# Two RMS norms of a hybrid encoder block taken from turned squares instead of ones-matmuls, and the memory keys projected token by token

## The chip, the cores and the metric

The kernel runs on one core of a Trainium2 chip. The metric is the device time of one execution in microseconds (us), and the median of several executions is compared. The kernel before took 859.05 us (median of three, 858.74 to 859.78). Times with one decimal or two in the text are counted from the start of the profiled span.

## What is computed

One encoder block, on 512 tokens of width 1024, with a memory of 256 tokens that one of its three mixers attends to. All arrays are float32. Cut to what matters here:

```python
h = rms_norm(x, mix_norm_g)                    # x: 512 x 1024
ml_q, ml_k, ml_v, ml_o, gates, na_qkv, xa_q, merge = split(h @ w_in)
y_ml = mlstm_branch(...); y_na = neighbourhood_attention(...)
mem_k, mem_v = split(rms_norm(mem, mem_norm_g) @ w_mem_kv, 2)   # mem: 256 x 1024, each 256 x 512
y_xa = memory_cross_attention(xa_q, mem_k, mem_v)
x = x + (gated sum of the branches) @ w_out
a, u = split(rms_norm(x, ffn_norm_g) @ w_up, 2)                 # 2 x 2816 columns
x = x + (gelu(dwconv3(a, w_conv, b_conv)) * u) @ w_down
return rms_norm(x, final_norm_g)
```

`rms_norm(x, g)` is `x * rsqrt(mean(x*x, -1) + 1e-6) * g`. The factor `rsqrt(...)` is one number per token.

## The kernel before

**Three matmuls for one.** Every product with weights is done in three passes of a rounded format: each operand is a rounded part and a rest, and `mm3` (lines 334 to 337) issues high by high, high by rest and rest by high. A weight block arrives from memory (`emit_raw`, L214, the tiles `wr`, three buffers of 512 KB), is split by ScalarE (rounded part, L301) and VectorE (rest, L302) into tiles `w`, two halves for a block and four halves in all, and is then used by TensorE. `weights(key)` issues the load of the block three ahead and the split of the block one ahead. All loads go through the queue of SyncE (SP), which issues in program order and stands still at a load whose buffer isn't free.

**The order.** Blocks are worked off in the order of `block_list`: the mLSTM queries and keys, the token-major values, then `xaq` (four blocks), `o` (four), `memk` (four), `memv` (four), `naq`, `nak`, the gates and branches, `out` (eight), then `ua` and `uu` in turn (22 of each: the "up stage"), then the down projection. In between, generators with the mLSTM chunks, the memory attention and the neighbourhood attention are stepped on, so that small matmuls stand among the large ones. A scheduler then orders the instructions of each engine, so that an instruction can be moved ahead of others that were written before it.

**Norms.** The activations are channel-major (a channel per partition, a token per column), so the sum of squares of a token goes across partitions. ScalarE squares, the squares are added into an accumulator (`macc` of 128x256 for the memory on VectorE, `acc2` of 128x512 ahead of the up stage on GpSimd, L1267). `rstd_parts` (L421 to L424) folds the two halves of the partitions and splits the sum into two rounded parts; `rstd_cols` sums over the partitions by a matmul with ones (L431), takes the diagonal out by VectorE (L435) for a column per 128 tokens, raises it to the power -0.5 on GpSimd (L438), and builds a diagonal matrix of it (L447, L448); `rstd_row` multiplies ones by that matrix (L454) and so has the factors as a row on all partitions, which ScalarE copies out (L456). The tile with the row is `rb`.

**Memory keys.** `memk` is projected channel-major: for each of four blocks of 128 key channels, 24 matmuls with the weights as the stationary operand and 256 memory tokens as columns; VectorE multiplies by the row (`to_mk`, L1167). The memory's values are projected token-major: the memory tokens are stationary, 512 value channels are the columns, and ScalarE scales by the column on the way out (L1186).

**Up stage.** For each of 22 `f`, `pa` (from `ua`) is multiplied by `rb` into a padded tile (L520), a convolution of three taps follows (L522 to L524), then the gelu (L1293 to L1296), a second multiplication by the row on GpSimd (L1298), and the product with `pu` (L1304 or L1306). The accumulators `mm` have four buffers in PSUM, `at` four others. The first blocks `ua 0`, `uu 0`, `ua 1`, `uu 1` are multiplied before the row is there.

**Turning.** `turn_out` transposes a 128x512 tile on VectorE in squares of 32x32 (L169) and writes it to a scratch tensor in four DMAs (L172, `td`), whose rows complete the transposition; `turn_in` (L178, `U`) reads it back. The tag `nab` has two buffers; the turned mLSTM keys are read into it (`U`, one load per head, used by the copies L763 and L764), and later the biases of the neighbourhood attention.

Of the kernel before, what the change touches and what calls it, by code (L numbers as in the profile page):

```python
# [11 lines left out]
F32 = mybir.dt.float32  # L12
# [109 lines left out]
BCOLS = {n: (lambda k: P) for n in ("mlk", "o", "xaq", "memk", "naq", "nak", "g", "out", "ua", "uu")}  # L122
BCOLS.update({n: (lambda k: 512) for n in ("mlq", "memv")})
# [7 lines left out]
def hybrid_block(ctx, tc, xT, memT, wflat, vecs, gbias, nabias, out):  # L131
# [34 lines left out]
    def turn_out(src):  # L166

        t = scr()
        V.transpose(t.rearrange("p (j s a) -> p s j a", j=4, s=4), src.rearrange("p s (j b) -> p s j b", j=4))  # L169
        d = dp.tile([P, S], F32, name=nm("td"))  # L170
        for i in range(4):
            SY.dma_start(d[:, i * P:(i + 1) * P].rearrange("(j b) c -> b j c", j=4),  # L172
                         t[32 * i:32 * i + 32].rearrange("b (j c) -> b j c", j=4))
        return d

    def turn_in(d, tag, bufs, plain=False):
        u = tp.tile([P, S], F32, tag=tag, name=nm("U"), bufs=bufs)
        SY.dma_start(u, d)  # L178
        return u if plain else u.rearrange("p (i s a) -> p s i a", i=4, s=4)
# [861 lines left out]
    def xa_all(xq, mk, mv, yh, yl):  # L1041
# [3 lines left out]
        def prep(h):  # L1045
            q, k = (rt(), rt()), rt()
            split_act(q[0], q[1], xq[:, h * S:(h + 1) * S])
            k = (k[:, :M], k[:, M:])
            split_act(k[0], k[1], mk[:, h * M:(h + 1) * M])
            return q, k  # L1050
# [101 lines left out]
    for f in range(4):  # L1152
        if f == 2:
            mp = rstd_parts(macc, M)
        ps = proj(("o", f), NH, NL, at=mid({4: lambda: norm.append(rstd_cols(mp, M, "m"))} if f == 3 else {}))
        if f == 0:
            so.append(unit())
        g = so[0][:, f * S:(f + 1) * S]
        A.activation(g.rearrange("p (i s a) -> p s i a", i=4, s=4), ps.rearrange("p (s i a) -> p s i a", s=4, i=4),
                     AF.Tanh, scale=0.5)  # L1160
        V.tensor_scalar(g, g, 1.0, None, op0=ALU.add)
        step(RB / 2)
    mrc = norm[2][0]
    mkv = unit()
    mk, mv = mkv[:, 0:1024], mkv[:, 1024:2048]
    def to_mk(f, ps):
        V.tensor_tensor(mk[:, f * M:(f + 1) * M], ps[:, :M], norm[3], op=ALU.mult)  # L1167
# [8 lines left out]
    pss = [mmps() for _ in range(2)]  # L1176
    for i in range(4):
        ws = weights(("memv", i))
        for t in range(2):
            tsl = slice(t * P, (t + 1) * P)  # L1180
            for k in range(2):
                kk = 2 * i + k
                mm3(pss[t], MH[kk][:, tsl], ML[kk][:, tsl], ws[k][0], ws[k][1], kk == 0, kk == KT - 1)
        step(RM)
    for t in range(2):
        A.activation(mv[:, t * 512:(t + 1) * 512], pss[t], AF.Copy, scale=mrc[:, t:t + 1])  # L1186
# [87 lines left out]
    for f in range(FT):  # L1274
        if f == 0:
# [6 lines left out]
            p2 = rstd_parts(acc2, S)  # L1282
# [181 lines left out]
def _layout(inp):  # L1464
# [14 lines left out]
    for key, n in BLOCKS:  # L1479
# [16 lines left out]
        elif kind == "memk":  # L1496
            b = mkv[:, :, key[1] * P:(key[1] + 1) * P]
# [64 lines left out]
```

## Time and profile before

| what | value |
|---|---|
| median of three executions | 859.05 us |
| profiled execution | 858.86 us |
| its span (first to last instruction) | 857.1 us |
| TensorE busy, as the profile models it | 99% of the span |
| VectorE, ScalarE, GpSimd busy | 71%, 53%, 17% |
| memory stage (`memk` and `memv`) | 146.57 to 174.57 us |
| start of the up stage on TensorE | 496.30 us |
| last matmul | 849.66 us |

A row of the timeline gives start, duration, engine, line, operation, output and inputs, their shapes and the count; in brackets stands the idle time of the engine before it and what ended it. A matmul's shown duration includes its way through the pipeline, so what one matmul costs in a row of many is the distance from start to start.

### The profile page before, as it was taken

Reading aid. Unit: us, or ns where it says so; the run is one execution under the profiler, and the core shown is the slowest. Engines: PE = TensorE matmul, PEld = TensorE weight load, DVE = VectorE, ACT = ScalarE, POOL = GpSimd, SP = SyncE. Lnnn points to the kernel's source line nnn. Section 1 sums busy time; section 2 is a strip of 40 time slices with the busy share of each in tenths; the row PEclk is TensorE's granted clock in tenths of the full one; section 3 lists DMA queues with packets and bytes.
Section 4 is the critical chain, followed back from the end, with each engine's and each line's share of the span. In section 5 each row is a group of like instructions: output and inputs, shape, how many; then the busy total and the mean of one; then the engine's idle time right before and its main releaser. Section 6 shows DMA issues by size and latency. Waiting matters only on the chain.

```text
span 857.1 us, 12198 instructions
## 1 busy us (share of the span) xinstructions
PE 848.7 (99%) x4056; PEld 714.0 (83%) x4056; DVE 606.4 (71%) x1218; ACT 458.2 (53%) x965; POOL 148.3 (17%) x234
## 2 busy tenths in 40 slices
PE   9999999999999999999999999999999999999996
PEld 7898988988888888888888888888888888888885
DVE  6699677865458658997586557767766667756763
ACT  7465556775446648887644435444444444533442
POOL 2000200000102830454000212111111112110201
PEclk9999999999999999999999999999999999999999
DMA  8236734543335856888623432444433233844842
GB/s 273 83 114 208 240 138 146 196 149 110 124 109 173 230 142 199 227 235 238 206 89 109 147 111 96 150 148 147 148 99 99 98 98 112 255 111 138 242 101 99
DMA packets 74815, 131.55 MB, mean 153 GB/s; under 512 B 9976, under 2 KB 34936, under 8 KB 74752
## 3 DMA queue, kind: packets, MB, share of 16 engines
q1 hardware_dynamic: 64944, 120.25, 43.3%
q0 software_dynamic: 9664, 10.51, 6.4%
q8 instruction: 32, 0.52, 0.2%
q14 instruction: 31, 0.25, 0.1%
q10 hardware_dynamic: 144, 0.00, 0.0%
HBM read 116.03 MB, written 14.70 MB: 153 GB/s over the span
## 4 chain that ended last, share of the span: by engine, by line
PE 99%; DVE 0%; issue 0%; POOLq 0%; POOL 0%; ACT 0%
PE mm L336 28%; PE mm L335 28%; PE mm L337 28%; PE at L335 3%; PE at L336 3%; PE at L337 3%; PE at L983 1%; PE at L816 1%; PE at L818 1%; PE at L800 1%; PE at L950 0%; PE at L949 0%; PE at L760 0%; PE at L367 0%; POOLq L1557 0%
## 5 line engine op out<-in xcount | busy, mean ns | idle before, releaser
L335 PE MATMUL mm<-u,w 128*128 128x512 f32 (+1 forms) x912 | 353.7, 388 | 0.0
L336 PE MATMUL mm<-u,w 128*128 128x512 f32 (+1 forms) x912 | 352.2, 386 | 0.0
L337 PE MATMUL mm<-u,w 128*128 128x512 f32 (+1 forms) x912 | 352.1, 386 | 0.0
L301 ACT ACTIVATE w<-wr 128x512 fp32r<-128x512 f32 (+1 forms) x256 | 159.8, 627 | 132.8 <-PE mm L337 103.6
L302 DVE TENSOR_TENSOR w<-wr,w 128x512 fp32r<-128x512 f32 (+2 forms) x257 | 175.9, 688 | 70.1 <-ACT w L301 67.8
L337 PEld LDWEIGHTS mm<-u,w 128*128 128x128 f32 x912 | 171.4, 188 | 34.9 <-DVE w L302 0.4
L335 PEld LDWEIGHTS mm<-u,w 128*128 128x128 f32 x912 | 171.7, 188 | 33.7 <-ACT u L341 0.3
L336 PEld LDWEIGHTS mm<-u,w 128*128 128x128 f32 x912 | 171.5, 188 | 33.6 <-DVE u L342 0.5
L629 POOL DMA_DIRECT2D u<-nav_d x128 | 62.1, 494 | 102.3 <-PE at L983 53.5
L1298 POOL TENSOR_TENSOR s<-s,rb 128x512 f32<-128x512 f32 x21 | 35.8, 1702 | 180.2 <-DVE s L1296 172.5
L238 ACT ACTIVATE w<-u 128x512 fp32r<-128x512 f32 x49 | 30.8, 631 | 55.5 <-PE mm L337 42.3
L335 PE MATMUL mm<-w,u 128*128 128x512 f32 x148 | 57.8, 390 | 0.0
L336 PE MATMUL mm<-w,u 128*128 128x512 f32 x148 | 57.6, 389 | 0.0
L337 PE MATMUL mm<-w,u 128*128 128x512 f32 x148 | 57.6, 389 | 0.0
L238 DVE TENSOR_TENSOR w<-u,w 128x512 fp32r<-128x512 f32 x49 | 33.8, 690 | 31.4 <-ACT w L238 30.9
L337 PEld LDWEIGHTS mm<-w,u 128*128 128x128 f32 x148 | 27.8, 188 | 5.8
L335 PEld LDWEIGHTS mm<-w,u 128*128 128x128 f32 x148 | 27.8, 188 | 5.7
L336 PEld LDWEIGHTS mm<-w,u 128*128 128x128 f32 x148 | 27.8, 188 | 5.6
L341 ACT ACTIVATE u<-s 128x512 fp32r<-128x512 f32 x14 | 8.9, 632 | 36.1 <-DVE s L1306 36.1
L522 ACT ACTIVATE s<-pad,vec 128x512 f32<-128x512 f32 x30 | 24.4, 812 | 5.3 <-DVE pad L520 4.4
L238 POOL DMA_DIRECT2D u<-wflat x16 | 14.0, 900 | 67.4 <-DVE u L238 22.4
L523 DVE SCALAR_TENSOR_TENSOR s<-pad,vec,s 128x512 f32<-128x512 f32 x30 | 22.5, 749 | 4.0 <-ACT s L522 4.0
(297 smaller groups left out, 1134.2 us busy)
## 6 DMA issues: line engine op xcount, KB each, us to landing
wr<-wflat SPq DMA_DIRECT2D x124, 512.0 KB, 3.4
u<-wflat SPq DMA_DIRECT2D x48, 256.0 KB, 4.9
td<-s SPq DMA_DIRECT2D x160, 64.0 KB, 1.9
U<-td SPq DMA_DIRECT2D x40, 256.0 KB, 3.6
s<-xT SPq DMA_DIRECT2D x24, 256.0 KB, 3.9
nab<-nabias SPq DMA_DIRECT2D x16, 256.0 KB, 4.3
u<-nav_d POOLq DMA_DIRECT2D x128, 32.0 KB, 3.5
u<-wflat POOLq DMA_DIRECT2D x16, 256.0 KB, 6.3
```

Source lines behind the costliest of these rows:

```text
L238: chain[eng] = getattr({"V": V, "A": A, "G": G}[eng], what)(*a, **k).ins
L301: A.activation(h[:, u:v], src, AF.Copy)
L302: V.tensor_tensor(l[:, u:v], src, h[:, u:v].bitcast(F32), op=ALU.subtract)
L335: PE.matmul(ps, lh, rh, start=start, stop=False)
L336: PE.matmul(ps, lh, rl, start=False, stop=False)
L337: st["mm"] = PE.matmul(ps, ll, rh, start=False, stop=stop).ins
L341: A.activation(h, src, AF.Copy, scale=scale)
L522: A.activation(t1, pad[:, 0:512], AF.Identity, scale=vcol(w, i), bias=vcol(b, i))
L523: V.scalar_tensor_tensor(t1, pad[:, 1:513], vcol(w, n + i), t1, op0=ALU.mult, op1=ALU.add)
L629: G.dma_start(vw[r * 32:(r + 1) * 32, i * 256:(i + 1) * 256], nav_v[hf, r, CW[b]:CW[b] + 32, hp * 256:(hp + 1) * 256])
L800: PE.matmul(pv[:, i, 0:129], kt[:, d, i], va[:, i + d, h, 0:129], start=True, stop=True)
L1298: chain["G"] = G.tensor_tensor(c, c, rb2, op=ALU.mult).ins
```

## The change

`turn_out` and `turn_in` take tiles of any number of 128-token groups. Two new functions take the norm's factors from turned squares: `rstd_turned` reduces the turned accumulator over its columns on VectorE (one number per token and group), adds the epsilon and raises to -0.5 on GpSimd; `rstd_row_turned` writes these columns to a scratch tensor and reads it back on all partitions. The norm of the memory and the norm ahead of the up stage use them; the first norm of the kernel still goes through the ones-matmuls. The memory keys are projected like the values, scaled by the column, turned, and read back into `mkv`; the copies in `prep` of the memory attention pick a head's keys out of the turned layout. `pa1` and `pu1` of the up stage go into banks of `at`.

```diff
-BCOLS = {n: (lambda k: P) for n in ("mlk", "o", "xaq", "memk", "naq", "nak", "g", "out", "ua", "uu")}
-BCOLS.update({n: (lambda k: 512) for n in ("mlq", "memv")})
+BCOLS = {n: (lambda k: P) for n in ("mlk", "o", "xaq", "naq", "nak", "g", "out", "ua", "uu")}
+BCOLS.update({n: (lambda k: 512) for n in ("mlq", "memk", "memv")})
...
+    def rstd_turned(u, tag):
+
+        nt = u.shape[1]
+        v, col = tiny(nt), cp.tile([P, nt], F32, name=f"rc_{tag}")
+        V.tensor_reduce(v, u, axis=AX.XY, op=ALU.add)
+        V.tensor_scalar(v, v, 1.0 / D, EPS, op0=ALU.mult, op1=ALU.add)
+        G.tensor_tensor(col, v, nhalf[:, :nt], op=ALU.pow)
+        return col
+
+    def rstd_row_turned(col, tag):
+
+        d = dp.tile([S], F32, name=nm("rd"))
+        SY.dma_start(d.rearrange("(t p) -> p t", p=P), col)
+        rb = cp.tile([P, S], F32, name=f"rb_{tag}", tag=f"rb{S}", bufs=2)
+        SY.dma_start(rb, d.partition_broadcast(P))
+        return rb
...
-            split_act(k[0], k[1], mk[:, h * M:(h + 1) * M])
+            ms = mk.rearrange("p (t i s a) -> p s t i a", t=2, i=4, s=4)[:, h]
+            kh, kl = [x.rearrange("p (t i a) -> p t i a", t=2, i=4) for x in k]
+            A.activation(kh, ms, AF.Copy)
+            V.tensor_tensor(kl, ms, kh.bitcast(F32), op=ALU.subtract)
...
     for f in range(4):
-        if f == 2:
-            mp = rstd_parts(macc, M)
-        ps = proj(("o", f), NH, NL, at=mid({4: lambda: norm.append(rstd_cols(mp, M, "m"))} if f == 3 else {}))
+        if f == 0:
+            md = turn_out(macc.rearrange("p (s b) -> p s b", s=2))
+        elif f == 1:
+            mt = turn_in(md, "nab", 2)
+        elif f == 2:
+            mrc = rstd_turned(mt, "m")
+        ps = proj(("o", f), NH, NL, at=mid())
...
-    ps_m = [proj(("memk", 0), MH, ML, M)]
-    step(RM)
-    for f in range(1, 4):
-        ps_m.append(proj(("memk", f), MH, ML, M, at={4: lambda: norm.append(rstd_row(norm[2][1], M, "m"))} if f == 1 else {}))
-        for i in range(2 if f == 1 else 1):
-            to_mk(f - 1 + i if f == 1 else f, ps_m.pop(0))
-        step(RM)
...
+    kd2 = []
+    for name in ("memk", "memv"):
+        pss = [mmps() for _ in range(2)]
+        for i in range(4):
+            ws = weights((name, i))
+            for t in range(2):
+                tsl = slice(t * P, (t + 1) * P)
+                for k in range(2):
+                    kk = 2 * i + k
+                    mm3(pss[t], MH[kk][:, tsl], ML[kk][:, tsl], ws[k][0], ws[k][1], kk == 0, kk == KT - 1)
+            step(RM)
+            if name == "memv" and i == 2:
+                for t in range(2):
+                    SY.dma_start(mk[:, t * 512:(t + 1) * 512], kd2[t])
         for t in range(2):
+            if name == "memk":
+                m = scr()
+                A.activation(m, pss[t], AF.Copy, scale=mrc[:, t:t + 1])
+                kd2.append(turn_out(by4(m)))
+            else:
+                A.activation(mv[:, t * 512:(t + 1) * 512], pss[t], AF.Copy, scale=mrc[:, t:t + 1])
...
-            p2 = rstd_parts(acc2, S)
+            t2 = turn_in(turn_out(by4(acc2)), "nab", 2)
...
-            pa1 = proj(("ua", 1), HH, HL, at={2: lambda: norm.append(rstd_cols(p2, S, "2"))})
-            pu1 = proj(("uu", 1), HH, HL, at={3: lambda: norm.append(rstd_row(norm[4][1], S, "2"))})
-            rb2 = norm[5]
+            pa1 = proj(("ua", 1), HH, HL, bank=atps)
+            rb2 = rstd_row_turned(rstd_turned(t2, "2"), "2")
+            pu1 = proj(("uu", 1), HH, HL, bank=atps)
```

The scheduler makes the following of it. First the queue of SP at the start of the up stage, before. `s_5340` is the last tile of `x`; the tiles `wr` are the loads of `ua 2`, `uu 2`, `ua 3`, `uu 3` and `ua 4`.

```order
L1258 DMA s_5340<-xT 128x512
L214 DMA wr_5391<-wflat 128x1024
L214 DMA wr_5455<-wflat 128x1024
L214 DMA wr_5514<-wflat 128x1024
L214 DMA wr_5575<-wflat 128x1024
L214 DMA wr_5619<-wflat 128x1024
```

The same place in the change. `s_5393` holds the transposed squares, `U_5400` is the turned accumulator, `gf` are the gains of the last norm, `rd_5446` the scratch tensor of the factors and `rb_5448` the row.

```order
L1282 DMA s_5290<-xT 128x512
L232 DMA wr_5341<-wflat 128x1024
L173 DMA td_5395<-s_5393 32x4x128 x4
L179 DMA U_5400<-td_5395 128x512
L232 DMA wr_5408<-wflat 128x1024
L1349 DMA gf_7194<-gbias 128x512
L1349 DMA gf_7196<-gbias 128x512
L194 DMA rd_5446<-rc_5442 128x4x1
L232 DMA wr_5450<-wflat 128x1024
L196 DMA rb_5448<-rd_5446 128x512
L232 DMA wr_5507<-wflat 128x1024
L232 DMA wr_5551<-wflat 128x1024
```

Four writes and one read of the turning, and the write and the read of the row, now stand among the weights. The two loads of the gains, which before stand in the queue at the neighbourhood attention (issued at 421.0 and 421.5 us), have moved here, since they share the tag `nab` with the turned squares.

Second, VectorE at the point where the row is first used, before. `pad` are the products with the row for `f` 0 and 1; `w_5577` and `w_5580` are the halves of `uu 2`, `w_5621` is the first half of `ua 3`.

```order
L302 TENSOR_TENSOR w_5577<-wr_5455,w_5577 128x512
L520 TENSOR_TENSOR pad_148<-mm_5399,rb_5537 128x512
L520 TENSOR_TENSOR pad_151<-mm_5463,rb_5537 128x512
L523 SCALAR_TENSOR_TENSOR s_5552<-pad_148,vec,s_5552 128x512
L524 SCALAR_TENSOR_TENSOR s_5552<-pad_148,vec,s_5552 128x512
L302 TENSOR_TENSOR w_5580<-wr_5455,w_5580 128x512
L1294 SCALAR_TENSOR_TENSOR s_5556<-s_5556,s_5552 128x512
L523 SCALAR_TENSOR_TENSOR s_5564<-pad_151,vec,s_5564 128x512
L1296 SCALAR_TENSOR_TENSOR s_5552<-s_5556,s_5552 128x512
L524 SCALAR_TENSOR_TENSOR s_5564<-pad_151,vec,s_5564 128x512
L1304 SCALAR_TENSOR_TENSOR u_5381<-mm_5400,s_5552 128x512
L302 TENSOR_TENSOR w_5621<-wr_5514,w_5621 128x512
```

In the change the halves of `uu 2` are `w_5509` and `w_5512`, and the first half of `ua 3` is `w_5553`.

```order
L538 TENSOR_TENSOR pad_148<-mm_5349,rb_5448 128x512
L538 TENSOR_TENSOR pad_151<-at_5416,rb_5448 128x512
L541 SCALAR_TENSOR_TENSOR s_5484<-pad_148,vec,s_5484 128x512
L320 TENSOR_TENSOR w_5509<-wr_5408,w_5509 128x512
L542 SCALAR_TENSOR_TENSOR s_5484<-pad_148,vec,s_5484 128x512
L1318 SCALAR_TENSOR_TENSOR s_5488<-s_5488,s_5484 128x512
L541 SCALAR_TENSOR_TENSOR s_5496<-pad_151,vec,s_5496 128x512
L320 TENSOR_TENSOR w_5512<-wr_5408,w_5512 128x512
L1320 SCALAR_TENSOR_TENSOR s_5484<-s_5488,s_5484 128x512
L542 SCALAR_TENSOR_TENSOR s_5496<-pad_151,vec,s_5496 128x512
L1328 SCALAR_TENSOR_TENSOR u_5331<-mm_5350,s_5484 128x512
L320 TENSOR_TENSOR w_5553<-wr_5450,w_5553 128x512
```

The first half of `uu 2` stood ahead of the two products with the row and stands behind them now: one more split lies between the row and `ua 3`.

Third, the queue of SP ahead of the memory stage, before. `U` are the turned keys of the mLSTM heads 2 and 3 (head 1's stand five rows earlier), `R` rows for its scans, and the `wr` are `o 3` and `memk 0` to `memk 3`.

```order
L214 DMA wr_1366<-wflat 128x1024
L738 DMA R_1302<-rd 128x512
L178 DMA U_1798<-td_562 128x512
L214 DMA wr_1402<-wflat 128x1024
L738 DMA R_1499<-rd 128x512
L214 DMA wr_1464<-wflat 128x1024
L738 DMA R_1503<-rd 128x512
L178 DMA U_2065<-td_610 128x512
L738 DMA R_1790<-rd 128x512
L214 DMA wr_1552<-wflat 128x1024
L214 DMA wr_1642<-wflat 128x1024
```

In the change, with `td_1368` and `U_1409` the turned squares of the memory, `U_1515`, `U_1742` and `U_2015` the keys of heads 1 to 3, and `wr_1411` to `wr_1560` the blocks `memk 0` to `memk 2`:

```order
L756 DMA R_1302<-rd 128x512
L173 DMA td_1368<-s_1366 32x4x64 x4
L232 DMA wr_1411<-wflat 128x1024
L756 DMA R_1507<-rd 128x512
L179 DMA U_1409<-td_1368 128x256
L232 DMA wr_1472<-wflat 128x1024
L756 DMA R_1511<-rd 128x512
L179 DMA U_1515<-td_514 128x512
L179 DMA U_1742<-td_562 128x512
L232 DMA wr_1560<-wflat 128x1024
L179 DMA U_2015<-td_610 128x512
L756 DMA R_1734<-rd 128x512
```

The turned squares take one of the two `nab` buffers, and the keys of heads 1 and 2 are now read behind them; the key of head 2 takes the buffer that the squares leave.

More of the change, by code (lines that the diff above doesn't have):

```diff
@@ L166, in turn_out @@
     def turn_out(src):
-        t = scr()
-        V.transpose(t.rearrange("p (j s a) -> p s j a", j=4, s=4), src.rearrange("p s (j b) -> p s j b", j=4))
-        d = dp.tile([P, S], F32, name=nm("td"))
+        n = src.shape[1]
+        t = scr(n * P)
+        V.transpose(t.rearrange("p (j s a) -> p s j a", j=4, s=n), src.rearrange("p s (j b) -> p s j b", j=4))
+        d = dp.tile([P, n * P], F32, name=nm("td"))
         for i in range(4):
-            SY.dma_start(d[:, i * P:(i + 1) * P].rearrange("(j b) c -> b j c", j=4),
+            SY.dma_start(d[:, i * n * 32:(i + 1) * n * 32].rearrange("(j b) c -> b j c", j=4),
                          t[32 * i:32 * i + 32].rearrange("b (j c) -> b j c", j=4))
@@ L176, in turn_in @@
     def turn_in(d, tag, bufs, plain=False):
-        u = tp.tile([P, S], F32, tag=tag, name=nm("U"), bufs=bufs)
+        u = tp.tile([P, S], F32, tag=tag, name=nm("U"), bufs=bufs)[:, :d.shape[1]]
         SY.dma_start(u, d)
-        return u if plain else u.rearrange("p (i s a) -> p s i a", i=4, s=4)
+        return u if plain else u.rearrange("p (i s a) -> p s i a", i=4, a=32)
+    def rstd_turned(u, tag):
[11 more added lines that the diff above has]
+        return rb
     def by4(a):
@@ L1496, in _layout @@
         elif kind == "memk":
-            b = mkv[:, :, key[1] * P:(key[1] + 1) * P]
+            b = mkv[:, 2 * key[1]:2 * key[1] + 2, :512]
         elif kind == "memv":
```

13 lines of the change are left out of this document (removed).

## The prediction

> **What bounds the kernel now.** I read the page's busy times and its chain first, then what TensorE waited for, then TensorE's timeline from start to start.
>
> ```profile
> PE 848.7 (99%) x4056; PEld 714.0 (83%) x4056; DVE 606.4 (71%) x1218; ACT 458.2 (53%) x965; POOL 148.3 (17%) x234
> ...
> PEclk9999999999999999999999999999999999999999
> ...
> PE 99%; DVE 0%; issue 0%; POOLq 0%; POOL 0%; ACT 0%
> ```
>
> The chain that ended last is TensorE for 99% of the span, and the granted clock is full throughout. Busy time alone would not say that TensorE has no gaps, because the ends of matmuls are modelled. The waits do:
>
> ```profile
> PE at L367 <- DVE warm L363: 1.2, 1, 1.2
> ```
>
> That is the whole answer for TensorE: it waited 1.2 us, at its first instruction. So neither norm costs a stall today, and what the change can win is TensorE's own work. What it can lose is any new wait of TensorE.
>
> The price of a matmul is the distance from one start to the next.
>
> ```profile
> 157.09 0.28 PE L336 MATMUL mm<-u,w 128*128 128x256 f32 x1
> ...
> 159.72 0.28 PE L337 MATMUL mm<-u,w 128*128 128x256 f32 x1
> ```
>
> ```profile
> 518.51 0.39 PE L335 MATMUL mm<-u,w 128*128 128x512 f32 x1
> ...
> 529.39 0.39 PE L335 MATMUL mm<-u,w 128*128 128x512 f32 x1
> ...
> 534.83 0.39 PE L335 MATMUL mm<-u,w 128*128 128x512 f32 x1
> ...
> 535.28 0.39 PE L337 MATMUL mm<-u,w 128*128 128x512 f32 x1
> ```
>
> The first two rows are the second and the last of a `memk` block's 24 matmuls: 22 steps in 2.63 us, 0.1195 us each for 256 columns. The rows below them are the first matmuls of `ua 2`, `ua 3` and `uu 3`, the last two 24 steps apart: 5.44 us, 0.2267 us each for 512 columns; the row at 535.28 is the third matmul of `uu 3`. Twice 0.1195 is 0.239, so a wide matmul saves 0.0123 us against two narrow ones.
>
> **The change part by part.** *Memory keys.* 4 x 24 = 96 matmuls of 256 columns become 4 x 12 = 48 of 512: 96 x 0.1195 = 11.47 us against 48 x 0.2267 = 10.88 us, **-0.59 us**. The small matmuls between the blocks stay where they were.
>
> The Trainium skill (TensorE: Matmul & The Clock Gate, "Back-to-back issue gap") gives an isolated gap of N/2.4 + 2.5 ns, so that halving the count would save only 48 x 2.5 = 0.12 us. By it, the keys would give -0.12 in place of -0.59; the two distances above leave some 13 ns per matmul here, not 2.5, and I take the trace.
>
> *Ones-matmuls.* Four go, two of 256 and two of 512 columns.
>
> ```profile
> 508.54 0.39 PE L431 MATMUL at<-s,onesr 128*128 128x512 f32 x1
> 508.76 0.39 PE L335 MATMUL mm<-u,w 128*128 128x512 f32 x1
> ```
>
> ```profile
> 152.22 0.28 PE L454 MATMUL at<-s,onesr 128*128 128x256 f32 x1
> 152.34 0.28 PE L335 MATMUL mm<-u,w 128*128 128x256 f32 x1
> ```
>
> Each takes its place in the row of matmuls and no more: 0.22 and 0.12. Together 2 x 0.227 + 2 x 0.12 = **-0.69 us**. The sum is -1.28 us.
>
> *What VectorE, ScalarE and GpSimd lose and gain* (folds, diagonals, `to_mk` out; transposes, two reductions, two key copies on ScalarE in) is worth nothing by itself: TensorE waited for none of them. It matters only where a weight half is split too late, which I follow at the two places where a new wait stands.
>
> *Up stage: when is the row there?* The last addition of squares, then the pieces of the turning as they are elsewhere in this trace:
>
> ```profile
> 498.09 1.29 POOL L1267 TENSOR_TENSOR acc<-acc,s 128x512 f32<-128x512 f32 x1 [4.07 <-ACT s L1266]
> ```
>
> ```profile
> L169 DVE STREAM_TRANSPOSE s<-s 128x512 f32<-128x512 f32 x24 | 16.9, 707 | 2.9 <-ACT s L962 2.2
> ...
> L1066 DVE TENSOR_REDUCE y<-at 128x2 f32<-128x512 f32 x8 | 5.5, 686 | 0.0
> ...
> L956 DVE TENSOR_SCALAR y<-y 128x2 f32<-128x2 f32 x16 | 2.6, 164 | 0.2
> ```
>
> ```profile
> 171.87 1.77 SPq L172 DMA_DIRECT2D td<-s  x4
> 173.73 0.38 SPq L214 DMA_DIRECT2D wr<-wflat  x1
> 175.25 0.34 SPq L178 DMA_DIRECT2D U<-td  x1
> ```
>
> ```profile
> 506.68 1.43 DVE L302 TENSOR_TENSOR w<-wr,w 128x512 fp32r<-128x512 f32 x2 [1.97 <-ACT w L301]
> ```
>
> ```profile
> 510.35 1.04 POOL L438 TENSOR_TENSOR rc<-y,nhalf 128x4 f32<-128x4 f32 x1 [10.97 <-DVE y L435]
> ```
>
> ```profile
> td<-s SPq DMA_DIRECT2D x160, 64.0 KB, 1.9
> U<-td SPq DMA_DIRECT2D x40, 256.0 KB, 3.6
> ...
> R<-rd SPq DMA_DIRECT2D x8, 256.0 KB, 3.8
> ...
> vec<-vecs SPq DMA_DIRECT2D x1, 86.0 KB, 6.2
> ...
> vec<-vecs ACTq DMA_DIRECT2D x1, 4.0 KB, 3.2
> ```
>
> The sum is complete at 498.09 + 1.29 = 499.4. The transpose ends at 500.2, the four writes and their landing take 175.25 - 171.87 = 3.4 (503.6), the read 3.6 (507.2). In the new order of VectorE the reduction stands between the two halves of `uu 1`, which are split at 506.68 and behind; so it runs at 507.4 and ends at 508.1, the second half is done at 508.8, the small addition at 509.0, the power at 510.1. Then the factors are written, in time X, and read back as a row; that is the kind of read `R` is (a row of 512 onto all partitions), 3.8 us. The row is used from 510.1 + X + 3.8 + 0.1 = 514.0 + X.
>
> X has no row of its own: 128 partitions with four single numbers each, written to places apart. Its bounds from the rows are 1.9 (`td`, 128 runs of 512 bytes) and four times that, 7.6, if each of the 512 numbers costs what a run of `td` costs. The nearest row by size and shape of run is the 4 KB transfer of 32 bytes per partition, 3.2 us; I take **X = 3.2**, the row at 517.2.
>
> The Trainium skill (DMA: Bandwidth & Descriptors, "Rules for kernel authors") says that a last dimension with strides becomes one descriptor per element and should be rearranged. That speaks against this write: 512 descriptors for 2 KB. No run so far shows such a transfer.
>
> *Until when may the row come?* Before:
>
> ```profile
> 516.41 1.28 DVE L520 TENSOR_TENSOR pad<-mm,rb 128x512 f32<-128x512 f32 x2
> ```
>
> ```profile
> 513.70 0.68 DVE L302 TENSOR_TENSOR w<-wr,w 128x512 fp32r<-128x512 f32 x1
> ```
>
> ```profile
> 530.97 0.68 DVE L302 TENSOR_TENSOR w<-wr,w 128x512 fp32r<-128x512 f32 x1
> ```
>
> The second row is the end of `ua 2`'s split. The row of factors is used first at 516.41, and behind it VectorE works without a long pause until the halves of `ua 3` and `uu 3` are split. The tightest is the first half of `uu 3`, done at 530.97 + 0.68 = 531.65 and wanted by its third matmul at 535.28: 3.6 us to spare. In the change that matmul comes 0.45 earlier (two ones-matmuls of this stage gone; what is gone earlier moves both alike), and one more split, 0.68, stands behind the row. So the row may be later than 516.41 by 3.6 - 0.45 - 0.68 = 2.5 us, that is at **518.9**, before TensorE waits. At 517.2 there are 1.7 us to spare: cost nothing. The accumulators don't decide: with `pa1` and `pu1` in `at`, `ua 2` and `uu 2` have their own banks, where before `ua 2` at 518.5 needed the bank that L520 frees at 517.1.
>
> SP stands still while it waits for X. Behind it is the load of `uu 3`, whose buffer isn't free before the split of `ua 2` (513.70 + 0.68 before), and whose use is 20 us off. It hides.
>
> *Memory stage.* The keys of head 2 now wait for the buffer of the turned squares, and on VectorE and ScalarE their copies stand ahead of the split of `memk 0`.
>
> ```profile
> 125.24 0.42 DVE L558 TENSOR_TENSOR acc_m<-acc_m,s 128x256 f32<-128x256 f32 x1
> ```
>
> ```profile
> 122.00:134.00 12.00, 12.00 (x61) 10.17 (x60) 10.05 (x26) 9.93 (x28) 0.00 (x0) 1.00 0.48 174
> ```
>
> ```profile
> 141.17 0.68 DVE L302 TENSOR_TENSOR w<-wr,w 128x512 fp32r<-128x512 f32 x1
> ```
>
> ```profile
> 146.57 0.36 PE L335 MATMUL mm<-u,w 128*128 128x256 f32 x1
> ```
>
> The sum is complete at 125.7. The window's columns are its length and then the busy time of TensorE, of its weight loads, of VectorE, ScalarE and GpSimd: VectorE is 10.05 of 12 us busy there, so I give the transpose until 127.5; writes 3.4, read 3.6, reduction 0.4: 135. The keys are read by 138.6 and copied by 139.5, when the split of `memk 0` began at 141.17 before anyway. It is wanted at 146.4, so some 5 us cover the new wait. The two folds, the diagonals and ScalarE's three small copies no longer stand ahead of `memk 1`. The keys' way back (two key copies, turning, read) ends some 10 us behind the last `memk`, at about 170, while the memory attention starts after `nak`. Cost nothing.
>
> **The sum.** 858.86 of the profiled execution, whose span is 857.1, less 1.28 is 857.6. The median of before is 0.19 above that execution, which would give 857.8. I predict 857.6.
>
> **Rivals.** *The row is late (slower).* Above X = 4.9 TensorE waits by the excess, at `uu 3`; at X = 6.2, which is what the slowest load on this queue took, the wait eats the 1.3 us; at X = 7.6 the row comes at 521.6, TensorE waits 2.7 and the time is 857.6 + 2.7 = 860.3. Against it speaks that 2 KB are moved; for it, that 512 separate numbers are written to memory, which nothing in this kernel did. Beyond X = 8 the kernel is slower by over 0.2%. Should each number cost three times as much as a run of `td`, X is 22.8, the row at 536.8, the wait 17.9 and the time 875.5.
>
> The Trainium skill (VectorE: DVE Perf Modes, "The three transpose paths") warns that a plain copy that transposes by strides is 19 times slower than the transposing path. By that figure on `td`'s 1.9 us X would be 36 us, an estimate, and the time near 889; no row here bears it out.
>
> *The memory's turning is late.* The two rows below are the least, the median and the longest landing of all writes of `td` and of all reads `U`.
>
> ```profile
> DMA to landing us min/median/max: 1.6/1.9/4.6
> ```
>
> ```profile
> DMA to landing us min/median/max: 2.6/3.6/5.5
> ```
>
> If one write of `td`, the read and the keys' read take their longest, the keys come 2.7 + 1.9 + 1.9 = 6.5 us later, at 145.1; their copies take 0.9 and the split 0.7, so the half is there at 146.7 where it is wanted at about 146.4. TensorE waits 0.3 to 0.4 us for `memk 0`: 858.0.
>
> *The matmuls don't get cheaper.* If the wide matmuls with the memory tokens as stationary operand were no better than two narrow ones, only the ones-matmuls would go: 858.2. The `memv` blocks already run this way at the distance of 0.2267, which speaks against it.
>
> **How the numbers follow.** Forecast without a new wait: 0.68, of which 0.18 lies beyond -0.2% (1.7 us; -1.28 is near that bound, and 0.2% is about what a measurement of this kernel tells from no change). Late row with X up to 7.6: 0.10, within 0.2%. Late row beyond that, up to three times a run and more: 0.14, slower. Memory's turning late: 0.06; matmuls no cheaper: 0.02; both within 0.2%. Faster 0.18, same 0.50 + 0.10 + 0.06 + 0.02 = 0.68, slower 0.14. The range goes from 1 us below the forecast (the spread of the three runs before) to the late row at X = 7.6: 856.6 to 860.3. It leaves out the case of 0.14.
>
> **What would show it.** In the profile of the changed kernel TensorE's answer on waits should still hold one entry; 48 matmuls of 512 columns should stand in `memk` at 0.2267 apart; each of the two ones-matmul lines should occur once; the write of the factors should land in about 3.2 us, and the products with the row start at about 517 less the 1 us gained earlier. A TensorE wait on VectorE's split at `uu 2` to `ua 4` would show the late row; one at the first `memk` block the late keys.

## The result and the profile after

The changed kernel takes 866.11 us (median of four, 865.47 to 867.87) beside 859.41 for the kernel before on the same chips: the ratio is 1.0081, with a 95% interval of 1.0069 to 1.0093. It is slower by 6.7 us. 857.6 was predicted, 856.6 to 860.3. The profiled execution took 867.87, its span is 866.1.

I read the same views in the same order. The chain that ended last of the changed kernel:

```profile
PE 94%; DMA 2%; issue 1%; DVE 1%; POOL 0%; ACT 0%; POOLq 0%; SPq 0%
```

TensorE is no longer the whole chain: 2% of it is transfers, in a kernel whose chain had none. Then what TensorE waited for (total, times, longest):

```profile
PE mm L353 <- ACT w L319: 5.5, 1, 5.5
PE at L385 <- DVE warm L381: 1.2, 1, 1.2
PE mm L355 <- DVE w L320: 0.9, 2, 0.5
```

The wait at the start is the old one. New is one wait of 5.5 us on ScalarE's half of a weight split, with two small ones on VectorE's half behind it. The next fences follow the first backwards: TensorE's timeline, ScalarE's, VectorE's and the queue of SP.

```profile
523.24 0.39 PE L355 MATMUL mm<-u,w 128*128 128x512 f32 x1
529.08 0.79 PE L353 MATMUL mm<-u,w 128*128 128x512 f32 x1 [5.45 <-ACT w L319]
529.67 0.63 PE L354 MATMUL mm<-u,w 128*128 128x512 f32 x1
530.10 0.65 PE L355 MATMUL mm<-u,w 128*128 128x512 f32 x1
```

```profile
527.69 0.81 ACT L540 ACTIVATE s<-pad,vec 128x512 f32<-128x512 f32 x1 [14.28 <-DVE pad L538]
528.41 0.61 ACT L319 ACTIVATE w<-wr 128x512 fp32r<-128x512 f32 x1
```

```profile
526.91 0.69 DVE L538 TENSOR_TENSOR pad<-mm,rb 128x512 f32<-128x512 f32 x1 [12.77 <-DMA rb<-rd]
```

```profile
510.44 0.38 SPq L194 DMA_DIRECT2D rd<-rc  x1
510.87 0.50 SPq L232 DMA_DIRECT2D wr<-wflat  x1
521.90 0.33 SPq L196 DMA_DIRECT2D rb<-rd  x1
```

The block `uu 2` starts 5.6 us after `ua 2` ends (523.24 + 0.23). Its weights are split at 528.41, because on ScalarE that split stands behind the convolution of `f` = 0 (L540), which waits for the product with the row (L538), which waits for the row until 526.9. And the row is late because its write is issued at 510.44 and the read only at 521.90. The landing times (last number, us from issue):

```profile
rb<-rd SPq DMA_DIRECT2D x1, 256.0 KB, 5.0
...
rd<-rc SPq DMA_DIRECT2D x1, 2.0 KB, 11.4
```

The 2 KB take 11.4 us to land. The weight load issued behind them at 510.87, that of `ua 3`, is slow too; it landed at 523.6, some 5 us before `ua 3` would have been due without the stall:

```profile
DMA to landing us min/median/max: 12.8/12.8/12.8
```

There is a second cost behind the wait. In these windows the column after the busy times is the granted clock:

```profile
523.00:529.00 6.00, 0.63 (x3) 0.19 (x1) 1.75 (x3) 1.31 (x2) 0.00 (x0) 0.97 0.47 133
529.00:532.00 3.00, 2.92 (x7) 2.16 (x8) 2.25 (x4) 1.38 (x4) 0.00 (x0) 0.50 0.01 3
532.00:536.00 4.00, 4.00 (x19) 3.31 (x18) 2.80 (x6) 2.18 (x4) 1.74 (x1) 1.00 0.39 120
```

For 3 us behind the stall the clock is at half: 7 matmuls where 13 fit at 0.2267. Those steps of 0.43 take 1.5 us more than steps of 0.2267. The Trainium skill (TensorE: Matmul & The Clock Gate, "What's actually happening") says that the clock falls to half after an idle window of some 3.4 us and comes back after a busy one of that length. This trace agrees, with 5.45 us idle and 3 us at 0.50; two runs below differ, where waits of 3.3 us (`write_act`) and 2.9 us (`pe_warm`) were enough.

Matched matmul by matmul with the kernel before, TensorE is 0.19 us late when `ua 2` begins and 9.0 us late at the last matmul. 8.8 us arise in the up stage: 5.6 at `uu 2`, 1.5 by the clock, and 1.5 at the third matmuls of `ua 3` and `uu 3` with the step behind each; some 0.2 are spread over slightly longer steps. That the 0.19 are not -1.28 comes mostly from this execution's first weights, on which TensorE goes in steps of 0.43 until 9.8 us (+1.36). In the profiled executions of the kernels below, whose first stage is the same, it lies between 0.1 us early and 1.4 late at that point: this part varies from one execution to the next.

### The profile page after: what moved, and what is told of

Same layout as the page of the kernel before. It is cut to its first block, busy times and chain, and to the rows that moved or that the text cites. A ratio compares the mean times of both kernels' runs of the same rounds, so it can differ in the third digit from the quotient of the medians.

```text
span 866.1 us, 12075 instructions
## 1 busy us (share of the span) xinstructions
PE 851.1 (98%) x4004; PEld 712.6 (82%) x4004; DVE 601.5 (69%) x1192; ACT 455.1 (53%) x955; POOL 149.0 (17%) x234
## 4 chain that ended last, share of the span: by engine, by line
PE 94%; DMA 2%; issue 1%; DVE 1%; POOL 0%; ACT 0%; POOLq 0%; SPq 0%
PE mm L355 27%; PE mm L353 27%; PE mm L354 27%; PE at L353 3%; PE at L354 3%; PE at L355 3%; DMA rd<-rc 1%; PE at L1001 1%; PE at L834 1%; PE at L836 1%; PE at L818 1%; DMA wr<-wflat 1%; PE at L967 0%; PE at L968 0%; PE at L778 0%
## 5 line engine op out<-in xcount | busy, mean ns | idle before, releaser
L353 PE MATMUL mm<-u,w 128*128 128x512 f32 x864 | 339.6, 393 | 5.7 <-ACT w L319 5.5
L355 PE MATMUL mm<-u,w 128*128 128x512 f32 x864 | 338.1, 391 | 0.9 <-DVE w L320 0.9
L354 PE MATMUL mm<-u,w 128*128 128x512 f32 x864 | 337.9, 391 | 0.0
L353 PEld LDWEIGHTS mm<-u,w 128*128 128x128 f32 x864 | 163.2, 189 | 39.0 <-ACT w L319 5.9
L355 PEld LDWEIGHTS mm<-u,w 128*128 128x128 f32 x864 | 162.8, 188 | 36.5 <-DVE w L320 2.4
L354 PEld LDWEIGHTS mm<-u,w 128*128 128x128 f32 x864 | 163.2, 189 | 33.4 <-DVE u L360 0.5
L353 PE MATMUL mm<-w,u 128*128 128x512 f32 x164 | 64.3, 392 | 0.0
L355 PE MATMUL mm<-w,u 128*128 128x512 f32 x164 | 63.8, 389 | 0.0
L354 PE MATMUL mm<-w,u 128*128 128x512 f32 x164 | 63.8, 389 | 0.0
L540 ACT ACTIVATE s<-pad,vec 128x512 f32<-128x512 f32 x30 | 24.3, 812 | 24.1 <-DVE pad L538 22.9
L355 PEld LDWEIGHTS mm<-w,u 128*128 128x128 f32 x164 | 30.8, 188 | 6.5
L354 PEld LDWEIGHTS mm<-w,u 128*128 128x128 f32 x164 | 30.8, 188 | 6.3
L353 PEld LDWEIGHTS mm<-w,u 128*128 128x128 f32 x164 | 30.8, 188 | 6.1
L538 DVE TENSOR_TENSOR pad<-mm,rb 128x512 f32<-128x512 f32 x21 | 14.5, 692 | 16.6 <-DMA rb<-rd 12.8
```

Of the source, the lines that this page charges most:

```text
L353: PE.matmul(ps, lh, rh, start=start, stop=False)
L354: PE.matmul(ps, lh, rl, start=False, stop=False)
L355: st["mm"] = PE.matmul(ps, ll, rh, start=False, stop=stop).ins
L538: V.tensor_tensor(pad[:, 1:513], ps, rbt, op=ALU.mult)
L540: A.activation(t1, pad[:, 0:512], AF.Identity, scale=vcol(w, i), bias=vcol(b, i))
```

## Experiments

All times are medians where no other number of executions is given. `mem_only`, `row16`, `write_act` and `pe_warm` ran beside the kernel before at 859.09; `runs128`, `write_twice`, `defer` and `defer_act` beside 858.96.

**The memory's part alone** (`mem_only`). The up stage has its old norm again:

```diff
-            t2 = turn_in(turn_out(by4(acc2)), "nab", 2)
+            p2 = rstd_parts(acc2, S)
...
-            pa1 = proj(("ua", 1), HH, HL, bank=atps)
-            rb2 = rstd_row_turned(rstd_turned(t2, "2"), "2")
-            pu1 = proj(("uu", 1), HH, HL, bank=atps)
+            pa1 = proj(("ua", 1), HH, HL, at={2: lambda: norm.append(rstd_cols(p2, S, "2"))})
+            pu1 = proj(("uu", 1), HH, HL, at={3: lambda: norm.append(rstd_row(norm[2][1], S, "2"))})
+            rb2 = norm[3]
```

> The memory's turned norm and the token-by-token keys stay, the up stage has its old norm with folds and ones-matmuls. Theory (the whole loss is the up stage's row of factors, which comes 9 us later than I took): nothing is left of the loss; TensorE has its wait at the start and no other, and the memory stage gains 0.59 by 48 wide matmuls and 0.24 by two ones-matmuls of 256 columns, so 0.8 us less than the kernel before, some 858.6 beside 859.4. Rival (the memory's part costs as well): TensorE waits in the memory stage, and the time is above 860.

Measured: 858.52, ratio 0.9993 (0.9985 to 1.0002). No wait in the memory stage; one of 0.5 us on the first weights, at 9 us. So the whole loss belongs to the up stage, and the memory's part is free of waits, as theory had it. The time by itself can't tell 0.8 us from nothing; the gain is read from rows. From the first small matmul ahead of the keys to the first of the values, in the kernel before and in the changed one:

```profile
144.43 0.38 PE L816 MATMUL at<-u,E 128*128 128x129 f32 x2
...
161.33 0.48 PE L335 MATMUL mm<-w,u 128*128 128x512 f32 x1
```

```profile
145.59 0.38 PE L834 MATMUL at<-u,E 128*128 128x129 f32 x2
...
161.82 0.48 PE L353 MATMUL mm<-w,u 128*128 128x512 f32 x1
```

16.90 against 16.23 us: 0.67 less, for the keys and one of the two ones-matmuls (0.71 predicted).

**The same 2 KB in longer runs** (`row16`). Each partition gets four neighbouring tokens, so that the factors lie in memory as 128 runs of 16 bytes:

```diff
-            t2 = turn_in(turn_out(by4(acc2)), "nab", 2)
+            t2 = turn_in(turn_out(acc2.rearrange("p (b s) -> p s b", s=4)), "nab", 2)
...
-        SY.dma_start(d.rearrange("(t p) -> p t", p=P), col)
+        SY.dma_start(d.rearrange("(p t) -> p t", p=P), col)
```

> As the changed kernel, but the up stage's squares are turned so that each partition holds the sums of four neighbouring tokens; the factors are then written as 128 runs of 16 bytes in place of 512 single numbers, the same 2 KB. Theory (the write is paid by the piece; 512 pieces took 11.4 us to land): 128 pieces land in 3 to 4 us, the row is used at about 518.5 where it was 526.9, no wait of TensorE is left, the weight load behind the write lands in under 6 us where it took 12.8, and the time is 858.1, 1.3 below the kernel before. Rival (the write is slow for its place in the queue, between loads): it still takes 8 us or more, and the time is above 862.

Measured: 857.99, ratio 0.9989 (0.9980 to 0.9998), 1.1 us less than the kernel before. Its waits, its two transfers and its first product with the row:

```profile
PE at L385 <- DVE warm L381: 1.2, 1, 1.2
```

```profile
rb<-rd SPq DMA_DIRECT2D x1, 256.0 KB, 4.4
...
rd<-rc SPq DMA_DIRECT2D x1, 2.0 KB, 2.7
```

```profile
516.97 0.69 DVE L538 TENSOR_TENSOR pad<-mm,rb 128x512 f32<-128x512 f32 x1 [4.12 <-DMA rb<-rd]
```

Two access patterns are all that differs, the orders of VectorE and ScalarE are the same, and TensorE has only its wait at the start. The shape of the write made the whole loss. That it is the number of pieces, as this expectation said, did not hold; the probes below show it.

**The write on another queue** (`write_act`). The write is issued by ScalarE:

```diff
-        SY.dma_start(d.rearrange("(t p) -> p t", p=P), col)
+        nc.scalar.dma_start(d.rearrange("(t p) -> p t", p=P), col)
```

> As the changed kernel, but the write of the 512 factors is issued on ScalarE's queue and not on SP's, so that no load stands before or behind it in its own queue. Theory (pieces): it still lands after about 11 us, the row is used at 526 to 527 and the time stays at 865 to 866; only the weight load that stood behind the write on SP's queue may land earlier. Rival (shared queue): the write lands in 2 to 4 us, and the time falls to about 858.

Measured: 865.16, ratio 1.0066 (1.0052 to 1.0079). The write, a window in which it is under way (last columns: clock, busy share of the DMA engines, GB/s), and the wait at `uu 2`:

```profile
rd<-rc ACTq DMA_DIRECT2D x1, 2.0 KB, 10.5
```

```profile
514.00:521.00 7.00, 7.00 (x32) 5.79 (x32) 0.02 (x1) 0.00 (x0) 0.00 (x0) 1.00 0.00 0
```

```profile
PE mm L353 <- ACT w L319: 3.3, 1, 3.3
```

Shared queue, the rival, is out. The window says more: while the write was outstanding, the DMA engines are recorded at a share of 0.00. They were not busy working off pieces then. They had done so before: from 510 to 514 us the record has 528 packets on this queue, and from 514 until the landing at 520.8 it has no packet of any queue.

```profile
q10 hardware_dynamic: 528, 0.00, 7.4%
```

So the 10.5 us lie for the most part between the last packet and the signal of the landing. The row came 2.2 us earlier than in the changed kernel (524.70), and TensorE's wait is 2.2 us shorter.

**The stall filled** (`pe_warm`). Matmuls whose result is overwritten keep TensorE going ahead of `uu 2`:

```diff
         ps = (bank or mmps)()
+        for _ in range(idle):
+            PE.matmul(ps, warm[:, :P], XHs[0], start=True, stop=True)
...
-            pu = pu1 if f == 1 else proj(("uu", f), HH, HL)
+            pu = pu1 if f == 1 else proj(("uu", f), HH, HL, idle=24 if f == 2 else 0)
```

> As the changed kernel, with 24 single matmuls of 512 columns put ahead of the block uu 2, into that block's own bank, which its first matmul then overwrites. They fill 5.4 of the 5.6 us in which TensorE stood still. Theory (the clock fell to half because TensorE stood still, and this cost 1.5 us behind the stall): uu 2 waits as long as before, but its first matmuls keep the distance of 0.2267, the granted clock stays 1.0 there, and the time is 1.5 us less than the changed kernel's, some 864.6. Rival (the clock falls there for another reason): the first matmuls of uu 2 stay 0.43 apart, and the time is 866.1 or more.

Measured: 868.28, ratio 1.0107 (1.0093 to 1.0120), more than either had said. TensorE's timeline at `uu 2` and at `uu 3`, and the windows around both:

```profile
521.95 5.75 PE L507 MATMUL mm<-u,warm 128*128 128x512 f32 x24
527.54 0.39 PE L353 MATMUL mm<-u,w 128*128 128x512 f32 x1
527.77 0.39 PE L354 MATMUL mm<-u,w 128*128 128x512 f32 x1
```

```profile
527.00:532.00 5.00, 5.00 (x24) 4.03 (x23) 4.05 (x7) 2.98 (x6) 0.76 (x1) 1.00 0.08 31
536.00:549.00 13.00, 10.07 (x37) 7.49 (x36) 10.05 (x15) 5.48 (x10) 3.33 (x2) 0.87 0.27 88
```

At `uu 2` theory holds: the block begins 5.6 us after the one before it, as in the changed kernel, but at a clock of 1.00 and in steps of 0.23. So it was the idleness that dropped the clock. The total is no test of it: the added matmuls made the scheduler put the split of `uu 3` behind the tanh of `f` = 2 on ScalarE, and TensorE then waited 2.9 us there and lost its clock at that place instead.

**Few long runs by a second turning** (`runs128`). VectorE turns the 128x4 factors once more, and they go out as 16 runs of 128 bytes:

```diff
+        V.tensor_scalar(wide[:, :NT], col, 1.0, None, op0=ALU.mult)
+        t = tiny(32)
+        V.transpose(t, wide)
+        for i in range(4):
+            SY.dma_start(d.rearrange("(t p) -> t p", p=P)[:, 32 * i:32 * i + 32], t[32 * i:32 * i + 4])
```

> As the changed kernel, with its tokens in their old places, but the 128x4 tile of factors is turned once more by VectorE (32x32 pieces), so that the same 2 KB go out as 16 runs of 128 bytes in four writes. Theory (pieces; 512 took 10.4 to 11.4 us, 128 took 2.7): each write lands in some 2 us as td does, the four issues add 1.5 us, the row is used at 517 to 518.5, no wait of TensorE, time about 858.0. Rival (the gain of the 128 runs came from tokens written in one stretch of memory, not from the number of pieces): the write still takes 8 us or more, time above 862.

Measured: 858.45, ratio 0.9993 (0.9983 to 1.0003), the row used at 518.28, no wait of TensorE beyond the first 10 us. It does what `row16` does, with the tokens in their old places, so the order of the tokens was not the point.

**The write issued twice** (`write_twice`), first to a place that nobody reads:

```diff
+        SY.dma_start(dp.tile([S], F32, name=nm("rd")).rearrange("(t p) -> p t", p=P), col)
         SY.dma_start(d.rearrange("(t p) -> p t", p=P), col)
```

> As the changed kernel, but the write of the 512 single factors is issued twice, first to a place that nobody reads, then to the one that the row is read from. Theory (pieces taken one behind the other, 20 ns each in all): the second lands 20 to 22 us behind the first's issue, the row is used at about 536, uu 2 waits 14 to 15 us in place of 5.5, and the time is about 875. Rival (10 us is a delay that each narrow write has, and two run beside each other): the second lands after 11 to 12 us, and the time is 866 to 867.

Measured: 864.69 in a single execution. The landing of the first and of the second write:

```profile
DMA to landing us min/median/max: 10.5/10.5/10.5
```

```profile
DMA to landing us min/median/max: 10.6/10.6/10.6
```

My theory falls here. Two times 512 pieces land side by side in the time of one, so they are not all worked off one behind the other.

**Where the pieces go** (`probe_far`, `probe_128`). What the two writes did not share is the memory that they go to. In each kernel an unread write stands ahead of the row's own:

```diff
+        far = dp.tile([S, P], F32, name=nm("far"))
+        SY.dma_start(far.rearrange("(t p) c -> p t c", p=P)[:, :, 0:1], col.rearrange("p (t c) -> p t c", c=1))
```

```diff
+        SY.dma_start(dp.tile([P, 1], F32, name=nm("one")), col[:, 0:1])
```

> The run with two writes showed 10.5 and 10.6 us side by side, so 512 pieces don't queue behind one another. Here the first, unread write puts its 512 numbers 512 bytes apart; the second is the row's own as before. Theory (pieces that fall into the same short stretch of memory, 128 of them to 512 bytes, are completed one behind the other, some 80 ns each): the far write lands in 2 to 4 us, the row's own still in 10.5. Rival (it is the number of pieces, 512, or 32 per DMA engine, wherever they go): the far write takes 10 us as well. The row comes as in the changed kernel, so the time is about 865 in both.

> As the changed kernel, with an unread write of the first 128 factors ahead of the row's own: 128 pieces of 4 bytes into one stretch of 512 bytes. Theory (pieces in one short stretch are completed one behind the other): it lands after about 10 us, as 512 pieces in four such stretches do. Rival (number of pieces): it lands in 2.7 us, as the 128 pieces of 16 bytes did. The time is about 865 in both.

Measured: 864.19 and 863.81, a single execution each, beside 859.85. First the kernel with the far write, then the one with 128 numbers:

```profile
far<-rc SPq DMA_DIRECT2D x1, 2.0 KB, 2.1
...
rd<-rc SPq DMA_DIRECT2D x1, 2.0 KB, 9.6
```

```profile
one<-rc SPq DMA_DIRECT2D x1, 0.5 KB, 8.3
rd<-rc SPq DMA_DIRECT2D x1, 2.0 KB, 9.7
```

512 single numbers 512 bytes apart land in 2.1 us. 128 single numbers side by side take 8.3. So the price is that many small pieces fall close together in memory. As an estimate, the whole landing comes to 65 to 90 ns for each of the 128 that share 512 bytes (8.3 / 128 and 11.4 / 128). That it grows with their number was not tried, nor how short the stretch is within which they hinder each other, and the 8.3 were measured with the row's own write issued 0.4 us behind, not alone. What keeps the pieces waiting stays open too; in `write_act` it comes after the DMA engines' recorded part.

**The products behind the splits** (`defer`). The slow write stays. An order is put on VectorE: the first two products with the row come after the first half of `ua 3` is split, and `ua 2` and `uu 2` are written ahead of the first convolution:

```diff
+        with tc.issue_after(vs[late]) if (late := (("ua", 3), 0)) in vs and w == "ffw" and i < 2 else ExitStack():
-        V.tensor_tensor(pad[:, 1:513], ps, rbt, op=ALU.mult)
+            V.tensor_tensor(pad[:, 1:513], ps, rbt, op=ALU.mult)
```

> As the changed kernel with its slow write, but on VectorE and ScalarE the first two products with the row stand behind the splits of uu 2 and of the first half of ua 3, where they stood ahead of them. Theory (TensorE stood because the split of uu 2 was queued behind the product, in an engine that works in order): the wait of 5.5 us at uu 2 shrinks to about 1, which is left because the weight load of uu 2 stands behind the slow write and landed at 523.7; the row still comes at about 527; some 1 to 2 us of waits come later, since the bank of uu 0 is freed only some 9.6 us after the row; the granted clock stays near 1.0; time about 861. Rival (TensorE waits for something else that needs the row, the banks of the accumulators first): uu 2 still waits 4 us or more, and the time is 864 or above.

Measured: 861.56 (859.90 to 862.82, eight runs), ratio 1.0027 (1.0016 to 1.0038). The waits of the profiled execution, which is its fastest:

```profile
PE mm L355 <- DVE w L320: 1.4, 2, 0.9
PE at L385 <- DVE warm L381: 1.2, 1, 1.2
```

The row still came at 524.8, and the 5.5 us at `uu 2` are gone; what is left is 1.4 us in VectorE's backlog, at 540 and 546. So it was the order on VectorE and ScalarE that made the late row a stall, not the banks. One reason in the expectation was wrong: the load that stands behind the write is that of `ua 3`, and `uu 2` doesn't wait for it. It landed 12.2 us after its issue, at 521.9, and it is ScalarE's split of `ua 3` that waits for it here:

```profile
522.04 0.63 ACT L319 ACTIVATE w<-wr 128x512 fp32r<-128x512 f32 x1 [4.32 <-DMA wr<-wflat]
```

With the products put behind that split, a late load now delays them as a late row does.

**The same with the write on the other queue** (`defer_act`), the one-line edit of `write_act` added.

> As the run with the products put behind the splits, and the write of the 512 factors is on ScalarE's queue. Theory (the slow write also holds up the load that stands behind it in its queue, 12.8 us against 4.6 with the write on the other queue): uu 2's weights land in under 6 us, uu 2 begins without any wait, the row comes at 524.7 and uu 3's bank is free when it is wanted; time 858 to 859. Rival (the load is not what is left): uu 2 waits about as long as in the run before, and the time is 860.5 or more.

Measured: 858.37, ratio 0.9994 (0.9984 to 1.0003), though the write takes 10.8 us. One wait is new:

```profile
PE mm L355 <- DVE w L320: 0.4, 1, 0.4
```

Here the load of `ua 3` was issued at 507.8, before the write, and landed in 4.6 us; the row came at 523.8. The profiled executions of the two differ by 1.1 us, the medians by 3.2. That the kernel holds the time of the mended ones with a write of 10.8 us shows the order's part once more; what the slower executions of `defer` wait for was not traced. For the load two things differ at once, the queue and the moment. So one more run.

**A load behind the write on another queue** (`other_queue`). The write is on ScalarE's queue, an unread load on SP's:

```diff
-        SY.dma_start(d.rearrange("(t p) -> p t", p=P), col)
+        nc.scalar.dma_start(d.rearrange("(t p) -> p t", p=P), col)
+        z = scr()
+        G.tensor_copy(z[:, :NT], col)
+        SY.dma_start(z, xT[:, 0, :])
```

> The slow write on ScalarE's queue, as before, and behind it in time an added load of 256 KB that nothing reads, on SP's queue; it is made to wait for the factors, so it is issued 1 to 2 us after the write. It tells whether a load behind the slow write is late because of the queue that it shares or because of the time at which it comes. Theory (a load issued behind the slow write is not done until the write is, whatever the queue): it lands 8 us or more after its issue, near the write's landing. Rival (only the write's own queue is held up): it lands in 3 to 5 us. The row and the time stay at about 865.

Measured: 864.29 in a single execution, beside 859.31. The write was issued at 510.32 and the load at 510.57. The first row below is the load's landing, the second the write's:

```profile
DMA to landing us min/median/max: 8.9/8.9/8.9
```

```profile
rd<-rc ACTq DMA_DIRECT2D x1, 2.0 KB, 8.9
```

Such loads take 4.6 in the median of this run; this one is done 0.2 us after the write. Its data had been moved long before (last columns: clock, share of the DMA engines, GB/s):

```profile
510.00:515.00 5.00, 5.00 (x24) 4.14 (x23) 1.39 (x2) 1.26 (x2) 0.47 (x2) 1.00 0.69 195
515.00:520.00 5.00, 5.00 (x24) 4.14 (x23) 0.00 (x0) 0.00 (x0) 0.00 (x0) 1.00 0.00 0
```

Nothing moves from 515 on, and the load counts as landed at 519.5. What is issued while the slow write is under way waits with it, on either queue; what is issued before it does not (in the same run the weight load at 509.12 landed in 4.8). On the write's own queue the data come slowly as well: 32 GB/s from 514 to 522 us in the changed kernel, where the load of `ua 3` was the only transfer left to move. The Trainium skill (DMA: Bandwidth & Descriptors, "Queues, rings and completion order") says that a transfer's completion signal lands only after every earlier write of that DMA engine, across its queues. These two landings agree with it; the slow data on the write's own queue are another matter, whose cause stays open.

## Why the prediction was wrong

**What failed is one term, X.** The prediction said "X has no row of its own", took 3.2 us from a load with 32-byte runs, and bounded the near case by 7.6, four times a write of `td`. It was 11.4 (8.9 to 11.4 in the runs with this pattern). Of the 9.7 us by which the row came later than 517.2, X is 8.2, the read 1.2 and the later issue of the write 0.3. "Written to places apart" is true of the four numbers of one partition, which lie 512 bytes apart; the numbers of neighbouring partitions lie side by side. Both ends were worked out per run or per number, from transfers whose runs lie 512 bytes or more apart, or that go into the chip. What priced this write is how close its pieces lie in memory, and no row of the kernel before had that. The range should have taken this in: the late row beyond 7.6 had a chance of 0.14, was priced at 875.5 alone, and stood outside.

**The rule behind it nearly held.** "Above X = 4.9 TensorE waits by the excess". I had counted the block starts three matmuls too late. In the kernel before, `ua 2` starts at 517.83, not 518.51, and the up stage at 495.6, not at 496.3 as the table says; in the changed kernel the change of bank shows the same start:

```profile
517.83 0.39 PE L335 MATMUL mm<-u,w 128*128 128x512 f32 x1
```

```profile
517.80 0.39 PE L355 MATMUL at<-u,w 128*128 128x512 f32 x1
518.02 0.39 PE L353 MATMUL mm<-u,w 128*128 128x512 f32 x1
```

By the same working the row may thus come at 518.2, not 518.9, in the times of the kernel before. In the changed kernel's profiled execution the up stage begins 0.6 us later, so the limit is 518.8. The row was used at 526.9: an excess of 8.1 us, and TensorE lost 8.8 in this stage. `write_act`, whose VectorE and ScalarE have the same order, has an excess of 6.0 and a loss of 6.5; `row16`, used before its limit, lost 0.1. 857.6 + 8.1 = 865.7; the median is 866.1.

Two details were off. The first and largest wait was not at VectorE's half of `uu 3` but at ScalarE's half of `uu 2`, where the convolution stands ahead of the split. And the half clock was not in the sum. It seems to have taken the place of later waits rather than to have come on top: in `write_act` the slow steps last about twice as long and the waits behind them are 0.3 us, not 1.5; its loss is no further from the excess. No run changes the clock alone, so this is not shown.

**TensorE's gain was right.** -0.59 for the keys and -0.69 for the ones-matmuls: in the changed kernel TensorE gained 0.81 us between the first stage and the values (0.83 predicted) and 0.45 in the up stage (0.45 predicted). With the write mended (`row16`) most of it shows: 1.1 us less in the median, with an interval of 0.2 to 1.7, where 1.28 were predicted.

**The memory's turning** cost nothing, as predicted.

**"SP stands still while it waits for X"**: it did, for 11 us, and the load of `uu 3` behind it hid, as predicted. What I had not seen is that a load already issued behind the write, that of `ua 3`, is slowed as well (12.8 us). It hid too, with some 4 us to spare once its split is counted.

**Descriptors and strides.** The Trainium skill's warning of one descriptor per element (DMA: Bandwidth & Descriptors, "Rules for kernel authors") gave the right advice here, and the trace agrees that the numbers went out one by one (the 528 packets of `write_act`). Their number is not what made the price: the far write has 512 single elements too and landed in 2.1 us. The Trainium skill's factor 19 (VectorE: DVE Perf Modes, "The three transpose paths") is stated for a large stride and against the chip's transposing DMA, which `td` is not, so the page does not give the prediction's 36 us; the write took 6 times `td`'s 1.9.

## What to carry to other kernels

Price a transfer by its pattern in memory before its bytes: 128 single numbers side by side took 8.3 us, 512 spread out 2.1, and the same 2 KB in runs of 16 bytes 2.7. If the trace has no transfer of that pattern, the unknown is open upwards, and the range must say so. A value that comes late costs nothing until an engine that works in order meets it ahead of work that TensorE wants: mend the transfer first, then look at what is queued behind its first use.

## What was not expected

- A write that lasts 10 us leaves the DMA engines idle in the record (0.00 over 7 us), and yet holds up what is issued while it is under way, on both queues (on its own, a weight load takes 12.1 to 12.9 us behind it and 4.6 to 4.8 ahead of it; on the other, a load of 256 KB took 8.9 where 4.6 is usual).
- Waits of 2.9 us (`pe_warm`) and 3.3 us (`write_act`) were enough to drop TensorE's clock; waits of 0.4 to 0.9 us and one of 2.1 (`other_queue`) left it at 1.00. The drop in `write_act`:

```profile
523.00:530.00 7.00, 3.69 (x11) 2.43 (x10) 4.30 (x7) 3.00 (x5) 0.00 (x0) 0.68 0.26 91
```

- Matmuls of no use, put into a stall, kept the clock up and still made the kernel slower, since the scheduler moved a split elsewhere for them.
